# Retention in a hybrid decoder layer: q times the carried state as one f32 matmul, the mean of squares on ScalarE, and a third raw weight buffer filled half a pair ahead

## The chip, the cores and the metric

The kernel runs on one core of one Trainium2 chip. The metric is the device time of one execution in microseconds (us), as the median of the runs of a kernel. The engines are named as in the profile: PE is TensorE, PEld its weight load, DVE is VectorE, ACT is ScalarE, POOL is GpSimd, SP is SyncE, which issues DMAs; each engine works through its own instructions in the order in which they stand.

## What is computed

The reference is one inference step of a layer with a windowed attention, a retention branch, a gated merge and a convolutional FFN, on a prompt of 1024 tokens and a group of 8 sequences with 4 new tokens each. The change lies in the retention branch and in the product with `w_in` that feeds it. Per head (4 of them, keys of 128, values of 256) and per block of 128 tokens:

```python
h = xn @ w_in                      # q, k, v, gates of all branches: the columns are split after
scores = einsum('bihd,bjhd->bhij', q, k) * dmask
inner  = einsum('bhij,bjhe->bihe', scores, v)
cross  = einsum('bihd,bhde->bihe', q, s0) * q_decay      # q times the carried state
s_new  = exp(log_g * L) * s0 + einsum('bjhd,bjhe->bhde', k * k_decay, v)
o      = inner + cross;  o = o * rsqrt(mean(o * o) + EPS)
```

The new tokens of the 8 sequences go through the same formula with a state of their own that comes from memory (`state_ret`) and goes back to it (`ret_sample`).

## The kernel before

All data are float32. Nearly every product is made from two-part operands of the type f32r: `split(hi, lo, src)` (L227) writes `hi`, a cast on ACT (L228), and `lo = src - hi` (L223 where DVE does it, L225 where POOL does), and `mm3` (L254 to 257) issues three matmuls, hi by hi, hi by lo, lo by hi. A few small products are f32 matmuls without a split; the trace shows each of those as two records.

Nothing in the change touches the first 290 us (norm, attention) or what follows about 700 us (merge, `w_o`, FFN). In between two streams of work run through each other:

- **The stream** (`stream`, L874). It makes 16 column pairs of `w_in` one after the other, by a Strassen-Winograd scheme: 7 products of 12 matmuls for each half `j` of the tokens, 14 a pair. A pair's raw weights are two loads of 512 KB, in `pair_weights` (L335; the DMAs are L340), the first holding a11 and a12, the second a21 and a22. `in_split` (L857) forms the sums (`s1` and `a21`, on DVE in L223) and splits all seven operands (`w_split`, L323: cast on ACT in L329, rest on DVE). The raw buffers come from the pool `wraw` with two buffers. `in_split` of the next pair is started, that is its loads are issued, at A22 of a pair's first half, and its operands are asked for one by one during the second half. Products leave PSUM by ACT (L898) and by two adds on DVE (L921, L923, tile `pair`).
- **The retention of the samples** (`sample`, L991), four heads, about 300 to 440 us. Per head it handles 8 states in 4 blocks of two: `load_s0` (L984; DMA L989) fetches a block, `split` makes `s0s`, four matmuls use it, `kb` (L1033) and L1035 make the update, L1036 adds it on DVE in place, and POOL issues the store (L1038). `load_s0` is called two blocks ahead of use, with four buffers.
- **The retention of the prompt**, 32 blocks `g` (4 heads of 8 blocks), about 440 to 700 us. `front` (L1108) makes k by q and turned k in `ps_a` (L1113, L1114), masks and splits the scores (`sT`), scales k (`kt`), splits `v` (`vt`) and, in all blocks but a head's first, splits q (`qs`, cast on ACT, rest on POOL). `middle` (L1130) adds scores by v and q by state in `ps_b` and makes k by v in `ps_a`; L1144 makes the new state on DVE, and the state is split (`sts`, ACT and DVE) for the next block. `finish` (L970) squares the output with a sum (L971, ACT), takes mean and eps on DVE (`ms`, L280), the power -1/2 on POOL (`rs`, L282), and scales on ACT (L973). `tail` (L1155) turns it by two matmuls (L979) and multiplies the gate in (L1163, DVE).

The code says in which order these are written (`adv(n)` takes n steps of the stream between two pieces of retention); the final order of each engine's instructions is set by a scheduler at build, which places them by its own estimates of durations. The loads of `w_raw`, of the states and of q and k stand in one queue, SP's, in a fixed order: a load that waits for its buffer holds all loads behind it.

Of the kernel before, what the change touches and what calls it, by code (L numbers as in the profile page):

```python
# [9 lines left out]
F32 = mybir.dt.float32  # L10
F32R = mybir.dt.float32r
U32 = mybir.dt.uint32
AF = mybir.ActivationFunctionType
# [5 lines left out]
P = 128  # L19
# [101 lines left out]
def trunk(ctx, tc, I, O):  # L121
# [645 lines left out]
    pb = ppool("pb", 2, ps_stack)  # L767
    wx["sum"], wx["raw"] = pool("wsum", 1, stack=sm_stack), wraw
    p2 = pool("p2", 1, stack=ph_stack)
# [38 lines left out]
    def ST(name, shape, dt=F32, **kw):  # L808
        return rp.tile(list(shape), dt, name=name, **kw)
# [64 lines left out]
    def stream():  # L874
# [3 lines left out]
        next(ws)  # L878
        ops = {p: next(ws) for p in early}
        last, nh = None, 0  # L880
        for i, n in enumerate(ORDER):
            for j in range(2):
# [17 lines left out]
                for p in (A11, S1, A22, S2, A12, S4, S3):  # L900
                    if p == A22:
                        if last is not None:
                            product(A22, *last)
                        if j == 0:
                            ops[A22] = next(ws)
                            if i + 1 < len(ORDER):
                                ws = in_split(ORDER[i + 1])
                                next(ws)
                        if last is not None:
                            yield  # L910
                        continue
# [14 lines left out]
                    if j and i + 1 < len(ORDER):  # L926
                        nxt[p] = next(ws)
                    yield
                last = bk[1], ops[A22], j, dst
# [37 lines left out]
    def finish(po, n, s, h, bufs=2):  # L967

        ssq = sml.tile([P, 1], F32, name="ss")[:n]
        o = ST("o", (P, 256), bufs=bufs)[:n]  # L970
        S.activation(o, po[:n, :256], AF.Square, accum_out=ssq)  # L971
        r = rsqrt_mean(ssq, 256, n, 1, oeps[:n, s, h:h + 1])
        S.mul(o, po[:n, :256], r)  # L973
        return o
# [9 lines left out]
    def load_s0(n):  # L984
        if n >= 2 * DB:
            return
        h, bb = n // 4, 2 * (n % 4)
        s0s_[n] = ST("s0", (P, 2, 256), bufs=4)
        ld.dma_start(out=s0s_[n], in_=I["state_ret"][0, bb:bb + 2, h].rearrange("b k e -> k b e"))  # L989

    def sample(h):  # L991
        gS = float(GAMMA[h] ** 4)
        dm = ST("dm", (P, P), bufs=2)
        ld.dma_start(out=dm, in_=I["dmask"][:, h, 1])
# [5 lines left out]
        for i in range(2):  # L1000
            S.copy(out=r8[:, i, :].rearrange("p (o t) -> p o t", o=4), in_=rep(qk8[:, i]))
        v8 = ST("v8", (P, 256), F32R, bufs=2)
        S.copy(out=v8[0:32], in_=vs)
# [17 lines left out]
        for bb in range(0, DB, 2):  # L1021
            s0 = s0s_[(h * DB + bb) // 2]
            load_s0((h * DB + bb) // 2 + 2)
            s0s = ST("s0s", (P, 2, 2, 256), F32R)
# [19 lines left out]

    for n in range(2):
        load_s0(n)
    adv(18)
# [60 lines left out]
    def front(g, dm):  # L1108
# [14 lines left out]
        split(vt[:, 0], vt[:, 1], f32(vt[:, 1]))  # L1123
        qs = None
        if tt:
            qs = ST("qs", (P, 2, P), F32R, bufs=2)
            split(qs[:, 0], qs[:, 1], q, G)
        return ps, sT, kt, vt, qs

    def middle(g, ps, sT, kt, vt, qs):  # L1130
        h, tt = divmod(g, NB)
# [5 lines left out]
        if tt:  # L1137
            sts = state["sts"]
            mm3(po, qs[:, 0], qs[:, 1], sts[:, 0], sts[:, 1], False, True)
        pk = ps[:, 256:]  # L1140
# [580 lines left out]
```

## Time and profile before

| what | value |
|---|---|
| median of 3 runs | 1690.79 us (1689.51 to 1692.35) |
| the profiled execution | 1689.79 us, its span 1688.0 us |
| mean granted clock of TensorE | 0.992 |
| busy over the span: PE, DVE, ACT, POOL | 97%, 75%, 52%, 30% |
| PE instructions | 12643 |

The span runs from the first to the last instruction; 1.79 us of the profiled execution lie outside it. Granted clock is what the throttle gave TensorE as a share of full speed. In the rows of the profile, `x28` is a count, three durations are minimum, median and maximum in ns, and `[1.66 <-DVE pair L921]` says that the engine stood idle for 1.66 us until that instruction of another engine had ended.

### The profile page before, as it was taken

To read this page: it belongs to the slowest core of one execution; us is meant where nothing else is said; L and a number is where in the kernel's file an instruction comes from. 1 tells how busy PE (TensorE), PEld (TensorE's weight loads), DVE (VectorE), ACT (ScalarE), POOL (GpSimd) and SP (SyncE) were. 2 spreads that over 40 slices of the span, in tenths; PEclk is the share of its full clock that TensorE was granted. 3 is DMA by queue.
4 is the path that set the end of the run, shared out by engine and by line. 5 is a ranking of instruction groups with operands and counts; after the bars stand their busy time and mean duration, and the time that the engine had idled before them with its cause. 6 is when DMAs were issued, how large, how long until landed. Compare 5 with 4: busy or idle time off the path is not lost.

```text
span 1688.0 us, 32984 instructions
## 1 busy us (share of the span) xinstructions
PE 1633.9 (97%) x12643; PEld 1591.9 (94%) x12643; DVE 1273.3 (75%) x2227; ACT 870.0 (52%) x1942; POOL 499.1 (30%) x714
## 2 busy tenths in 40 slices
PE   8999999888989999999899999999999999999997
PEld 7999989888989989999778999999999999999997
DVE  7887737799677777658857888888888888445476
ACT  6566534444656665564433555555555556444343
POOL 4232420356344443341312122212313323111101
PEclk9999999999999999999999999999999999999999
DMA  7212222435777677596721244454444447866655
GB/s 198 66 45 73 82 63 103 147 124 168 225 230 230 202 246 222 194 296 205 229 94 68 64 141 159 150 161 148 152 146 146 146 146 254 256 184 201 196 175 157
DMA packets 273295, 273.92 MB, mean 162 GB/s; under 512 B 23040, under 2 KB 234272, under 8 KB 273121
## 3 DMA queue, kind: packets, MB, share of 16 engines
q1 hardware_dynamic: 239377, 155.25, 31.7%
q0 software_dynamic: 33760, 116.57, 19.9%
q8 instruction: 99, 1.62, 0.4%
q14 instruction: 59, 0.48, 0.1%
HBM read 184.24 MB, written 87.49 MB: 161 GB/s over the span
## 4 chain that ended last, share of the span: by engine, by line
PE 74%; DVE 9%; DMA 8%; issue 3%; ACT 3%; POOL 1%; SPq 0%; DVEq 0%; ACTq 0%; POOLq 0%
PE ps_m L256 9%; PE ps_m L257 9%; PE ps_m L255 9%; PE ps_t L256 7%; PE ps_t L255 7%; PE ps_t L257 7%; PE ps_q L255 3%; PE ps_q L257 3%; PE ps_q L256 3%; PE ps_mm L255 3%; PE ps_mm L256 3%; PE ps_mm L257 3%; DMA w_raw<-in_w_in 2%; DVE w L223 1%; DMA w_raw<-in_w_r_proj 1%
## 5 line engine op out<-in xcount | busy, mean ns | idle before, releaser
L255 PE MATMUL ps_q<-xh,w 128*128 128x264 f32 x512 | 150.6, 294 | 10.0 <-DVE pair L921 6.4
L223 DVE SCALAR_TENSOR_TENSOR w_lo<-w_raw,w_hi 128x1024 fp32r<-128x1024 f32 x83 | 104.8, 1268 | 65.8 <-ACT w_hi L228 61.3
L255 PE MATMUL ps_t<-xh,w_hi 128*128 128x264 f32 (+2 forms) x524 | 148.9, 284 | 0.0
L256 PE MATMUL ps_t<-xl,w_hi 128*128 128x264 f32 (+2 forms) x524 | 148.7, 284 | 0.0
L257 PE MATMUL ps_t<-xh,w_lo 128*128 128x264 f32 (+2 forms) x524 | 148.0, 283 | 0.0
L256 PE MATMUL ps_q<-xl,w 128*128 128x264 f32 x512 | 147.0, 287 | 0.0
L257 PE MATMUL ps_m<-xh,w_lo 128*128 128x264 f32 x512 | 145.5, 284 | 1.5 <-DVE w_lo L223 1.5
L257 PE MATMUL ps_q<-xh,w 128*128 128x264 f32 x512 | 146.3, 287 | 0.0
L255 PE MATMUL ps_m<-xh,w_hi 128*128 128x264 f32 x512 | 145.9, 285 | 0.0
L256 PE MATMUL ps_m<-xl,w_hi 128*128 128x264 f32 x512 | 145.5, 284 | 0.0
L223 DVE SCALAR_TENSOR_TENSOR w<-w_raw,w 128x512 fp32r<-128x512 f32 x152 | 110.3, 730 | 26.4 <-ACT w L329 25.3
L1471 DVE SCALAR_TENSOR_TENSOR c_out<-u_ext,fconst,c_out 128x1024 f32<-128x1024 f32 x96 | 122.0, 1281 | 2.6 <-ACT c_out L1467 0.5
L228 ACT CAST w_hi<-w_raw 128x1024 fp32r<-128x1024 f32 x62 | 65.2, 1051 | 107.0 <-PE ps_t L256 74.5
L255 PEld LDWEIGHTS ps_q<-xh,w 128*128 128x128 f32 x512 | 97.8, 191 | 12.9 <-DVE pair L921 8.4
L329 ACT CAST w<-w_raw 128x512 fp32r<-128x512 f32 x152 | 94.1, 621 | 27.0 <-DVE w_raw L223 15.1
L257 PEld LDWEIGHTS ps_t<-xh,w_lo 128*128 128x128 f32 x524 | 98.8, 188 | 0.0
L256 PEld LDWEIGHTS ps_t<-xl,w_hi 128*128 128x128 f32 x524 | 98.6, 188 | 0.0
L255 PEld LDWEIGHTS ps_t<-xh,w_hi 128*128 128x128 f32 x524 | 98.6, 188 | 0.0
L257 PEld LDWEIGHTS ps_m<-xh,w_lo 128*128 128x128 f32 x512 | 96.3, 188 | 1.9 <-DVE w_lo L223 1.9
L256 PEld LDWEIGHTS ps_q<-xl,w 128*128 128x128 f32 x512 | 97.9, 191 | 0.0
L257 PEld LDWEIGHTS ps_q<-xh,w 128*128 128x128 f32 x512 | 97.6, 191 | 0.0
L223 DVE SCALAR_TENSOR_TENSOR xl<-t,xh 128x1056 fp32r<-128x1056 f32 (+1 forms) x53 | 67.7, 1280 | 39.0 <-ACT xh L228 38.9
(468 smaller groups left out, 6233.2 us busy)
## 6 DMA issues: line engine op xcount, KB each, us to landing
w_raw<-in_w_up SPq DMA_DIRECT2D x48, 512.0 KB, 4.1
w_raw<-in_w_in SPq DMA_DIRECT2D x42, 512.0 KB, 4.6
w_raw<-s_d SPq DMA_DIRECT2D x60, 256.0 KB, 3.7
t_d<-t POOLq DMA_DIRECT2D x24, 528.0 KB, 4.1
t<-t_d POOLq DMA_DIRECT2D x24, 528.0 KB, 5.0
t<-in_w_down SPq DMA_DIRECT2D x40, 256.0 KB, 4.6
s_d<-t POOLq DMA_DIRECT2D x20, 512.0 KB, 3.7
w_raw<-in_w_down SPq DMA_DIRECT2D x36, 256.0 KB, 4.9
```

The costliest lines, as they stand in the source:

```text
L223: pinned(V.scalar_tensor_tensor(out=out, in0=in0, scalar=1.0, in1=in1, op0=mult, op1=op))
L228: pinned(S.copy(out=hi, in_=src))
L255: TE.matmul(ps, wh, xh, start=start, stop=False, **kw)
L256: TE.matmul(ps, wh, xl, start=False, stop=False, **kw)
L257: TE.matmul(ps, wl, xh, start=False, stop=stop, **kw)
L329: S.copy(out=t[:, 0:4], in_=src)
L1471: V.scalar_tensor_tensor(out=c[:, NS:], in0=u[:, g, NU + t:NU + t + SEQ], scalar=sc[t], in1=c[:, NS:], op0=mult, op1=add)
```

## The change

- The product of q and the carried state is one f32 matmul on the tiles `q` and `state` themselves; `qs`, `sts` and their splits are gone. That takes 84 f32r matmuls, 56 casts on ACT, 28 subtractions on DVE and 28 on POOL out, and puts 28 f32 matmuls in.
- In `finish` the squares are taken of a sixteenth of the values, so the sum is a mean over 256 already; eps is added by an ACT instruction in place of the one on DVE (36 of each). The power on POOL stays.
- Every third load of a `w_in` pair now lands in a buffer of the pool `wsum`, so there are three raw buffers. `in_split` is started for the pair after the next one, at S4 of a pair's second half, and once more before the loop.
- In `sample`, `s0` has three buffers instead of four and is fetched one block ahead instead of two; `dm` and `v8` have one buffer instead of two.

```diff
-    wx["sum"], wx["raw"] = pool("wsum", 1, stack=sm_stack), wraw
+    wx["sum"] = wx["raw"] = pool("wsum", 1, stack=sm_stack)
...
+        coming = in_split(ORDER[1])
+        next(coming)
...
                         if j == 0:
                             ops[A22] = next(ws)
-                            if i + 1 < len(ORDER):
-                                ws = in_split(ORDER[i + 1])
-                                next(ws)
+                            ws = coming
...
                     if j and i + 1 < len(ORDER):
                         nxt[p] = next(ws)
+                        if p == S4 and i + 2 < len(ORDER):
+                            coming = in_split(ORDER[i + 2])
+                            next(coming)
...
-        S.activation(o, po[:n, :256], AF.Square, accum_out=ssq)
-        r = rsqrt_mean(ssq, 256, n, 1, oeps[:n, s, h:h + 1])
+        S.activation(o, po[:n, :256], AF.Square, scale=1 / 16, accum_out=ssq)
+        ms = sml.tile([P, 16], F32, name="ms")[:n, :1]
+        S.activation(ms, ssq, AF.Identity, bias=oeps[:n, s, h:h + 1])
+        r = sml.tile([P, 16], F32, name="rs")[:n, :1]
+        G.tensor_tensor(out=r, in0=ms, in1=mhalf[:n, :1], op=ALU.pow)
...
-        s0s_[n] = ST("s0", (P, 2, 256), bufs=4)
+        s0s_[n] = ST("s0", (P, 2, 256), bufs=3)
...
-        dm = ST("dm", (P, P), bufs=2)
+        dm = ST("dm", (P, P))
...
-        v8 = ST("v8", (P, 256), F32R, bufs=2)
+        v8 = ST("v8", (P, 256), F32R)
...
-            load_s0((h * DB + bb) // 2 + 2)
+            load_s0((h * DB + bb) // 2 + 1)
...
-    for n in range(2):
-        load_s0(n)
+    load_s0(0)
...
-        qs = None
-        if tt:
-            qs = ST("qs", (P, 2, P), F32R, bufs=2)
-            split(qs[:, 0], qs[:, 1], q, G)
-        return ps, sT, kt, vt, qs
+        return ps, sT, kt, vt, q
...
-            sts = state["sts"]
-            mm3(po, qs[:, 0], qs[:, 1], sts[:, 0], sts[:, 1], False, True)
+            TE.matmul(po, q, state["s"], start=False, stop=True)
...
-        if tt < NB - 1:
-            sts = state["sts"] = ST("sts", (P, 2, 256), F32R)
-            split(sts[:, 0], sts[:, 1], ns_)
-        else:
+        if tt == NB - 1:
```

The scheduler's order differs from about 290 to 700 us on every engine, and nowhere else. Three places follow, each before and then after.

SP's queue where the stream begins: `w_raw` are the raw weights of the first pairs, `rcos` and `rsin` the tables of the rotation, `s_` the first sample states. Before:

```order
L340 DMA w_raw<-in_w_in 128x8x128
L956 DMA oeps<-in_oeps 128x8
L956 DMA kdec<-in_kdec 128x8
L340 DMA w_raw<-in_w_in 128x8x128 x3
L949 DMA rcos<-in_rcos 128x1056
L950 DMA rsin<-in_rsin 128x1056
L956 DMA bm<-in_bm 128x8
L989 DMA s_3562<-in_state_ret 128x2x256
L989 DMA s_3564<-in_state_ret 128x2x256
```

After:

```order
L340 DMA w_raw<-in_w_in 128x8x128
L959 DMA oeps<-in_oeps 128x8
L959 DMA kdec<-in_kdec 128x8
L340 DMA w_raw<-in_w_in 128x8x128 x4
L952 DMA rcos<-in_rcos 128x1056
L953 DMA rsin<-in_rsin 128x1056
L959 DMA bm<-in_bm 128x8
L995 DMA s_3562<-in_state_ret 128x2x256
L1000 DMA dm<-in_dmask 128x128
```

Five weight loads instead of four stand ahead of the tables, and one state load instead of two behind them.

DVE at the same place: `w_` are split operands, `s_3699` (after: `s_3697`) is the second pair's `s1`, `pair` the adds of the products (L921, L923). Before:

```order
L223 SCALAR_TENSOR_TENSOR w_3586<-w_raw,w_3586 128x512
L923 TENSOR_TENSOR pair<-ps_q_3596,pair 128x264
L223 SCALAR_TENSOR_TENSOR w_3700<-w_raw,w_3700 128x512
L921 TENSOR_TENSOR pair<-ps_q_3595,pair 128x264
L223 SCALAR_TENSOR_TENSOR s_3699<-w_raw 128x512
L822 STREAM_SHUFFLE sh<-pair 128x528
L223 SCALAR_TENSOR_TENSOR w_raw<-w_raw 128x512
```

After:

```order
L223 SCALAR_TENSOR_TENSOR w_3584<-w_raw,w_3584 128x512
L223 SCALAR_TENSOR_TENSOR s_3697<-w_raw 128x512
L923 TENSOR_TENSOR pair<-ps_q_3598,pair 128x264
L223 SCALAR_TENSOR_TENSOR w_raw<-w_raw 128x512
L223 SCALAR_TENSOR_TENSOR w_3698<-w_raw,w_3698 128x512
L921 TENSOR_TENSOR pair<-ps_q_3597,pair 128x264
L822 STREAM_SHUFFLE sh<-pair 128x528
```

The sums over the second pair's raw weights moved ahead of both adds on the first pair's products.

PE at the prompt's sixth block, with `ps_b<-vt,sT` scores by v, `ps_a<-vt,kt` k by v, `ps_a<-qk` k by q, `ps_q` the stream's products and L979 the turning of an output. Before, from the product of the fifth state on:

```order
L255 MATMUL ps_b<-vt,sT 128x256
L256 MATMUL ps_b<-vt,sT 128x256
L257 MATMUL ps_b<-vt,sT 128x256
L255 MATMUL ps_b<-sts,qs 128x256
L256 MATMUL ps_b<-sts,qs 128x256
L257 MATMUL ps_b<-sts,qs 128x256
L256 MATMUL ps_q_5959<-xl,w_5894 128x264
L257 MATMUL ps_q_5959<-xh,w_5894 128x264
L979 MATMUL ps_b<-ident,o 128x128 x2
L1113 MATMUL ps_a<-qk 128x128
L1114 MATMUL ps_a<-ident,qk 128x128
L255 MATMUL ps_a<-vt,kt 128x256
```

After:

```order
L255 MATMUL ps_b<-vt,sT 128x256
L256 MATMUL ps_b<-vt,sT 128x256
L257 MATMUL ps_b<-vt,sT 128x256
L1139 MATMUL ps_b<-state,qk 128x256
L255 MATMUL ps_a<-vt,kt 128x256
L256 MATMUL ps_a<-vt,kt 128x256
L257 MATMUL ps_a<-vt,kt 128x256
L255 MATMUL ps_b<-vt,sT 128x256
L256 MATMUL ps_b<-vt,sT 128x256
L257 MATMUL ps_b<-vt,sT 128x256
L1139 MATMUL ps_b<-state,qk 128x256
L255 MATMUL ps_a<-vt,kt 128x256
```

The three matmuls on `sts` and `qs` became the one of L1139. Two blocks now follow each other with no matmul of the stream between them, while before the stream's matmuls stood between one block and the next.

More of the change, by code (lines that the diff above doesn't have):

```diff
@@ L1123, in front, with middle @@
         split(vt[:, 0], vt[:, 1], f32(vt[:, 1]))
-        qs = None
-        if tt:
-            qs = ST("qs", (P, 2, P), F32R, bufs=2)
-            split(qs[:, 0], qs[:, 1], q, G)
-        return ps, sT, kt, vt, qs
-    def middle(g, ps, sT, kt, vt, qs):
+        return ps, sT, kt, vt, q
+    def middle(g, ps, sT, kt, vt, q):
         h, tt = divmod(g, NB)
```

## The prediction

> **What bounds the kernel now.** I read the page first, then busy times by stage, then what PE waits for in the stretch that the change reorders, then the places behind the largest of those waits.
>
> ```profile
> PE 1633.9 (97%) x12643; PEld 1591.9 (94%) x12643; DVE 1273.3 (75%) x2227; ACT 870.0 (52%) x1942; POOL 499.1 (30%) x714
> ```
>
> PE is busy for 97% of the span, so what can be won is the rest and the matmuls themselves. The stages, with the columns from, to, length, busy PE, PEld, DVE, ACT, POOL (instructions), granted clock, DMA share, GB/s:
>
> ```profile
> 290.00:420.00 130.00, 115.78 (x874) 110.91 (x873) 112.91 (x187) 52.93 (x129) 66.46 (x56) 0.97 0.44 144
> 420.00:700.00 280.00, 267.89 (x2155) 262.78 (x2154) 203.92 (x519) 166.55 (x457) 117.06 (x188) 0.99 0.70 221
> 320.00:360.00 40.00, 36.82 (x277) 36.05 (x277) 37.90 (x67) 16.22 (x44) 20.89 (x17) 0.93 0.42 136
> 360.00:400.00 40.00, 36.38 (x279) 33.94 (x278) 39.64 (x66) 17.58 (x47) 26.29 (x23) 1.00 0.43 138
> 480.00:520.00 40.00, 36.88 (x282) 35.95 (x282) 30.16 (x79) 23.54 (x67) 20.44 (x35) 0.91 0.71 223
> ```
>
> The affected 410 us hold two regimes. From 320 to 400 us, with the samples, DVE is full (37.90 and 39.64 of 40 us) and PE waits for it. From 420 on, DVE has slack on average (203.92 of 280) and PE waits now and then. Beside that, the granted clock costs 7% of 40 us (2.8 us) and 9% of 40 us (3.6 us) in two slices. PE's waits between 290 and 700 us (total, times, longest):
>
> ```profile
> PE ps_q L255 <- DVE pair L921: 6.4, 8, 1.7
> PE ps_a L1035 <- DVE kb L1033: 4.5, 5, 1.6
> PE ps_a L1113 <- DVE state L1144: 4.0, 3, 2.1
> PE ps_q L255 <- ACT pair L898: 3.7, 4, 1.3
> PE ps_b L979 <- ACT o L973: 2.7, 4, 0.9
> PE ps_q L255 <- DVE pair L923: 2.6, 2, 1.9
> ```
>
> These six sum to 23.9 us. That is the ceiling for everything the change does to waits; the halved clock could add some 6 us. Four of the six end on DVE, so the reader should ask what holds DVE there. One such place, DVE and then PE:
>
> ```profile
> 525.84 0.21 DVE L280 TENSOR_SCALAR ms<-ss,oeps 128x1 f32<-128x1 f32 x1
> 528.31 0.69 DVE L223 SCALAR_TENSOR_TENSOR s<-w_raw 128x512 f32<-128x512 f32 x1 [2.27 <-DMA w_raw<-in_w_in]
> 528.92 0.42 DVE L223 SCALAR_TENSOR_TENSOR sts<-state,sts 128x256 fp32r<-128x256 f32 x1
> 529.26 0.69 DVE L223 SCALAR_TENSOR_TENSOR w_raw<-w_raw 128x512 f32<-128x512 f32 x1
> 529.86 0.43 DVE L921 TENSOR_TENSOR pair<-ps_q,pair 128x264 f32<-128x264 f32 x1
> 530.34 0.39 PE L255 MATMUL ps_q<-xh,w 128*128 128x264 f32 x1 [1.66 <-DVE pair L921]
> ```
>
> PE's row names L921, but L921 was only queued: ahead of it DVE stood 2.27 us for a raw weight load, then did three other operations. The chain of waits has that load as its piece:
>
> ```profile
> 523.31 4.98 DMA w_raw<-in_w_in
> ```
>
> **Part 1: one f32 matmul for q times state.** The operations that go, by tile, and the durations that I use for the matmul:
>
> ```profile
> L228 ACT CAST sts<-state x28: 402/406/418, 462.8 to 691.6; 128x256 fp32r<-128x256 f32 x28
> L223 DVE SCALAR_TENSOR_TENSOR sts<-state,sts x28: 409/420/736, 463.7 to 692.0; 128x256 fp32r<-128x256 f32 x28
> L228 ACT CAST qs<-qk x28: 284/296/322, 454.3 to 684.2; 128x128 fp32r<-128x128 f32 x28
> L225 POOL TENSOR_TENSOR qs<-qk,qs x28: 447/475/1354, 454.7 to 684.6; 128x128 fp32r<-128x128 f32 x28
> 488.24 0.38 PE L1113 MATMUL ps_a<-qk 128*128 128x128 f32 x2
> 488.46 0.27 PE L1114 MATMUL ps_a<-ident,qk 128*128 128x128 f32 x1
> 488.70 0.28 PE L255 MATMUL ps_a<-vt,kt 128*128 128x256 f32 x1
> 488.81 0.28 PE L256 MATMUL ps_a<-vt,kt 128*128 128x256 f32 x1
> 488.93 0.28 PE L257 MATMUL ps_a<-vt,kt 128*128 128x256 f32 x1
> ```
>
> On PE, f32r matmuls of 256 columns start 0.115 to 0.12 us apart, so three cost 0.35. The f32 matmul of 128 columns is a pair of records: 0.38 for both against 0.27 for one, so they start 0.11 apart, and the next instruction starts 0.22 after the first. Twice the columns, twice that: 0.44. The product becomes dearer by 0.09 us, 28 x 0.09 = **+2.5 us**, all of it on the busiest engine. Bounds: if each of the two passes ran at the f32r pace, 2 x 0.118 = 0.24, -3.1 us; if each took its whole recorded 0.28, 0.56, +5.9 us. I take 0.44 since the row is the same kind of matmul.
>
> The Trainium skill, "FP8 and Floating Point Precision", section TensorE Precision Notes, counts a true FP32 product as four passes where the rounded form reads once, which speaks against replacing three matmuls by one: by it 4 x 0.118 = 0.47, and this term would be +3.4 us (an estimate). No row here has 256 columns in f32; the pair of L1113 is near the rule, for its two records are 0.11 apart at half the columns.
>
> On the others: DVE loses 28 x 0.420 = 11.8 us, ACT 28 x (0.406 + 0.296) = 19.7 us, POOL 28 x 0.475 = 13.3 us. None of these bounds, so the removal counts only through waits (part 2).
>
> **Part 2: the mean of squares on ACT.** What goes from DVE, and who waits in that chain:
>
> ```profile
> L280 DVE TENSOR_SCALAR ms<-ss,oeps x36: 195/208/217, 360.6 to 699.0; 128x1 f32<-128x1 f32 x32, 32x1 f32<-32x1 f32 x4
> ACT o L973 <- POOL rs L282: 10.2, 12, 2.3
> ```
>
> DVE loses 36 x 0.208 = 7.5 us. ACT gains 36 small instructions; I take the same 0.21 us, so 7.6 us (bounds from half of it to the cast's 0.406, 4 to 15 us), less than the 19.7 that part 1 took from it. The sum no longer stands behind DVE's queue on its way to POOL.
>
> Together DVE has 19.3 us less of 203.9, mostly in 420 to 700 us. The waits that this can shorten are those on the state (4.0) and on the scaled output (2.7). Both are chains of several engines, and only the queueing in them shrinks; I take a bit under half, **-3 us**, bounds 0 and -6.7. It could turn into a loss where blocks now follow each other on PE without cover (the sixth and seventh): 14 matmuls of the stream stood between them, 14 x 0.12 = 1.7 us, and without them PE waits for state and output once more, 2 to 3 us with the update (0.42) and the steps of `finish`. Before, this neighbourhood already cost a wait of that size and the slow clock of 480 to 520, so I set it off against those.
>
> **Part 3: third raw buffer, loads half a pair ahead.** The loads take 4.6 us to land in the median, and DVE waits for them:
>
> ```profile
> w_raw<-in_w_in SPq DMA_DIRECT2D x42, 512.0 KB, 4.6
> DVE s L223 <- DMA w_raw<-in_w_in: 15.0, 9, 3.0
> ```
>
> Nine waits, 15.0 us of DVE. A load that is issued half a pair (14 products x 12 matmuls x 0.12 / 2 = 10 us) earlier is there in time by more than its 4.6 us. What DVE's wait is worth on PE is read at 528: 2.27 became 1.66. Not every one lands on PE; the rows to which it can belong are those on L921 and L923, 6.4 + 2.6 = 9.0 us, the bound. I take a bit under half, **-4 us**, bounds 0 and -9. What is late next is L898 on ACT (3.7 us), which the change leaves.
>
> At the start of the stream the sums over the second pair now stand ahead of both adds:
>
> ```profile
> 301.66 0.43 DVE L923 TENSOR_TENSOR pair<-ps_q,pair 128x264 f32<-128x264 f32 x1 [1.32 <-PE ps_q L257]
> 307.77 0.69 DVE L223 SCALAR_TENSOR_TENSOR s<-w_raw 128x512 f32<-128x512 f32 x1 [3.04 <-DMA w_raw<-in_w_in]
> ```
>
> The 3.04 us of idle DVE come right before the stretch where DVE is full, so less of it moves all that follows forward; against that, L923, and with it the product that needs its bank, is now queued behind a load. SP's five loads instead of four delay the tables little, for the added buffer is free and its load has no wait. **-1 us**, bounds -3 and +1.5.
>
> **Part 4: what pays for the buffer.** A state block is fetched one block ahead with three buffers. The load for block m+1 now needs the store of block m-2 where it needed that of m-3. The third head's updates, and SP's waits for such stores:
>
> ```profile
> 409.06 0.68 DVE L1036 SCALAR_TENSOR_TENSOR s<-s,ps_a 128x512 f32<-128x512 f32 x1
> 413.05 0.67 DVE L1036 SCALAR_TENSOR_TENSOR s<-s,ps_a 128x512 f32<-128x512 f32 x1
> 417.06 0.68 DVE L1036 SCALAR_TENSOR_TENSOR s<-s,ps_a 128x512 f32<-128x512 f32 x1
> SPq L989 <- DMA out_ret_sample<-s: 40.4, 10, 9.8
> out_ret_sample<-s POOLq DMA_DIRECT2D x12, 256.0 KB, 3.1
> s<-in_state_ret SPq DMA_DIRECT2D x16, 256.0 KB, 2.7
> ```
>
> Update 0.7, store 3.1, load 2.7 and, as an estimate, 1.2 us for what waits in POOL's and SP's queues make 7.7 us from an update to the next load in its buffer. Two blocks are 8.0 us apart here: it just fits, with nothing to spare where there were 4 us. I take **+1 us**, bounds -3 (other order, same work) and +6 (rival 2).
>
> **Part 5: the clock.** The 2.8 and 3.6 us of lost clock come with the gaps; if gaps go, some of it goes. **-1.5 us**, bounds 0 and -6.4.
>
> Sum: +2.5 - 3 - 4 - 1 + 1 - 1.5 = **-6.0 us** on the profiled 1689.8 (span 1688.0 and 1.8 outside it). That execution lies 1.0 below the median of the runs, so I put it on the median: 1690.8 - 6.0 = **1684.8 us**. The forecast's own range is -10 to -3.
>
> **The rivals.** A measurement here can tell about 0.2%, 3.4 us, from no change.
>
> 1. *The gain stays in the queues.* SP's loads stand in one queue, and a load of q and k whose buffer is taken holds `w_raw` behind it, however many buffers there are:
>
> ```profile
> SPq L1084 <- PE ps_a L1114: 67.0, 22, 7.9
> ```
>
> Then part 3 gives -1, not -5, the freed DVE time stays idle time (-1, not -3), and parts 1, 4 and 5 (+2.5 + 1 - 1) make about 0: 1691 us. For it: 22 such waits. Against: the order puts the weight loads earlier in that queue.
>
> 2. *Slower: the states come late.* If store and load take 10 instead of 7.7 us (SP's longest wait was 9.8), each block waits 2 us from a spacing of 8.0 for two blocks on; DVE, which PE waits for there, loses about 1 us a block, 8 us over the last two heads, and the weight loads behind SP's wait are late as well, so part 3 gives -3. With +2.5 from part 1 and -2 from part 2, 1690.8 + 5.5 = about 1696 us. It decides from the point where the turn of a buffer takes more than two blocks' spacing. Against it: in the first two heads the spacing is wider, since DVE is full.
>
> 3. *More is won.* If all waits on L921 and L923 go (-9), those on state and output go (-6.7) and the clock comes back by half (-3), with +2.5 and +1: -15, 1676 us. For it speaks that delays on in-order queues add up. The Trainium skill, "SBUF — State Buffer", section Who interferes with whom, says that a DVE instruction with two SBUF inputs contends with a GpSimd instruction that reads SBUF; by it each of POOL's 28 removed subtractions could also have held DVE for up to its 0.475 us, 13 us of DVE. The trace agrees in one row: 736 ns at most for an `sts` subtraction whose median is 420.
>
> **How the numbers follow.** Forecast 0.48, rival 1 0.22, rival 2 0.18, rival 3 0.12. Of the forecast about 0.05 falls inside 3.4 us. So faster 0.43 + 0.12 = 0.55, same 0.22 + 0.05 = 0.27, slower 0.18. The range leaves out rival 3's far half and rival 2's far half, 0.15, and reaches from 1675 to 1696 us.
>
> **What would show it.** In the profile after: L1139's records 0.2 to 0.23 us apart (part 1 right); DVE's wait for `w_raw` down from 15.0 to under 5 us and PE's on L921 and L923 from 9.0 to about 5 (part 3); PE's waits on state and output below 6.7 together (part 2). ACT or DVE waiting for `in_state_ret` over 3 us would mean rival 2; SP still letting `w_raw` go late, rival 1. The forecast is wrong if 440 to 700 us takes as long as before.

## The result and the profile after

The changed kernel is slower: 1702.43 us (median of 8 runs, 1697.56 to 1709.54) against 1689.74 (8 runs, 1686.78 to 1692.35), a ratio of 1.0077 with a 95% interval of 1.0058 to 1.0095, some 13 us. The time lies above the predicted range. The profiled execution of the changed kernel took 1698.26 us; it is the second fastest of the eight and shows only 8.2 us of span more than before (1696.2 against 1688.0), so the size of the whole loss is taken from the timed runs, and the places from the profile.

```profile
PE 1633.4 (96%) x12615; PEld 1591.4 (94%) x12615; DVE 1255.0 (74%) x2163; ACT 867.6 (51%) x1922; POOL 487.1 (29%) x686
```

DVE lost 18.3 us of work, as the prediction worked out (19.3), POOL 12.0, and PE's busy time is the same. The work went as planned; the span did not follow. Where the time went is seen from when each thing happens. k turned (the transpose in `front`, 32 blocks) and the last of the stream's products, in the kernel before and then after ("456.3 to 686.8" are the first and the last start in us):

```profile
L1114 PE MATMUL ps_a<-ident,qk x32: 271/273/421, 456.3 to 686.8; 128*128 128x128 f32 x32
L257 PE MATMUL ps_q<-ex,w x256: 278/284/392, 291.7 to 726.0; 128*128 128x264 f32 x128
```

```profile
L1119 PE MATMUL ps_a<-ident,qk x32: 272/272/421, 463.5 to 693.5; 128*128 128x128 f32 x32
L257 PE MATMUL ps_q<-ex,w x256: 278/285/473, 291.8 to 732.9; 128*128 128x264 f32 x128
```

Both start the stream together, the prompt's first block comes 7.2 us later, and both streams of work end 6.7 to 6.9 us later. So most of the 8.2 us arise between 290 and 730 us, and they show first at the first head. PE there, three slices of 40 us (their columns as in the prediction), before and then after:

```profile
440.00:480.00 40.00, 38.22 (x311) 37.36 (x311) 27.74 (x70) 25.48 (x70) 15.59 (x26) 1.00 0.72 227
480.00:520.00 40.00, 36.88 (x282) 35.95 (x282) 30.16 (x79) 23.54 (x67) 20.44 (x35) 0.91 0.71 223
520.00:560.00 40.00, 37.32 (x305) 36.55 (x303) 29.47 (x77) 22.38 (x63) 17.61 (x28) 1.00 0.83 263
```

```profile
440.00:480.00 40.00, 37.52 (x296) 37.06 (x295) 22.63 (x52) 24.23 (x61) 11.62 (x19) 0.96 0.59 190
480.00:520.00 40.00, 32.08 (x240) 30.70 (x239) 26.44 (x69) 21.58 (x62) 17.55 (x28) 0.96 0.75 228
520.00:560.00 40.00, 39.52 (x322) 39.10 (x321) 28.42 (x69) 24.15 (x64) 13.86 (x22) 1.00 0.80 253
```

In the slice from 480 PE is busy for 32.08 us where it was 36.88: nearly 5 us are lost in the first head's later blocks, and some 2 of them come back in the slice from 520. PE's waits after, between 290 and 720 us:

```profile
PE ps_a L1118 <- DMA qk<-qk_d: 8.4, 3, 5.3
PE ps_q L255 <- DVE pair L921: 4.9, 4, 1.8
PE ps_a L255 <- DVE kt L1126: 2.6, 2, 1.4
PE ps_a L1118 <- DVE state L1144: 2.4, 3, 1.3
PE ps_q L255 <- DVE pair L923: 2.1, 2, 1.9
PE ps_b L985 <- ACT o L979: 1.3, 1, 1.3
```

The waits the change was to shorten did shrink: on state and scaled output together 3.7 us after 6.7, on L921 and L923 7.0 after 9.0. A wait that the profile of before did not show at all, on the loads of q and k, is larger than all of that.

The first of these three waits goes back to SP's queue, before and then after:

```profile
435.22 2.86 SPq L1084 DMA_DIRECT2D qk<-qk_d  x3
452.30 0.37 SPq L340 DMA_DIRECT2D w_raw<-in_w_in  x1
```

```profile
453.57 0.37 SPq L340 DMA_DIRECT2D w_raw<-in_w_in  x1
454.04 3.60 SPq L1089 DMA_DIRECT2D qk<-qk_d  x3
```

A weight load that must wait for its buffer until 453.57 now stands ahead of the first three q/k loads, which are issued 19 us later than before. PE pays 2.48 us at once, and 5.29 in a later block:

```profile
462.94 0.77 PE L1118 MATMUL ps_a<-qk 128*128 128x128 f32 x2 [2.48 <-DMA qk<-qk_d]
496.68 0.77 PE L1118 MATMUL ps_a<-qk 128*128 128x128 f32 x2 [5.29 <-DMA qk<-qk_d]
```

That second load stands in SP's queue behind the loads of the table `w_down`, which wait for a buffer, and DVE stands for the same table:

```profile
489.24 1.37 SPq L292 DMA_DIRECT2D zt<-in_w_down  x2
490.66 1.21 SPq L1089 DMA_DIRECT2D qk<-qk_d  x2
```

```profile
496.10 1.35 DVE L223 SCALAR_TENSOR_TENSOR zt<-zt 128x256 f32<-128x256 f32 x3 [5.66 <-DMA zt<-in_w_down]
```

```profile
DVE s L223 <- DMA w_raw<-in_w_in: 29.1, 12, 5.5
```

The last line, of DVE's waits from 290 to 720 us, bears on part 3 of the prediction: DVE's wait for raw weights nearly doubled, from 15.0 to 29.1 us, with three buffers and earlier loads.

### The profile page after: what moved, and what is told of

Same layout as the page of the kernel before. It is cut to its first block, busy times and chain, and to the rows that moved or that the text cites. A ratio compares the mean times of both kernels' runs of the same rounds, so it can differ in the third digit from the quotient of the medians.

```text
span 1696.2 us, 32758 instructions
## 1 busy us (share of the span) xinstructions
PE 1633.4 (96%) x12615; PEld 1591.4 (94%) x12615; DVE 1255.0 (74%) x2163; ACT 867.6 (51%) x1922; POOL 487.1 (29%) x686
## 4 chain that ended last, share of the span: by engine, by line
PE 56%; DMA 9%; DVE 5%; issue 4%; ACT 2%; POOL 1%; SPq 0%; DVEq 0%; POOLq 0%; ACTq 0%
PE ps_m L256 8%; PE ps_m L257 8%; PE ps_m L255 8%; PE ps_t L256 7%; PE ps_t L255 7%; PE ps_t L257 7%; PE ps_q L257 2%; PE ps_q L255 2%; PE ps_q L256 2%; DMA qk<-qk_d 1%; DMA vt<-v_d 1%; DMA t<-z_d 1%; DMA g_in<-gm_d 1%; DMA zt<-in_w_r_proj 1%; DVE w L223 1%
## 5 line engine op out<-in xcount | busy, mean ns | idle before, releaser
L255 PE MATMUL ps_q<-xh,w 128*128 128x264 f32 x512 | 149.3, 292 | 7.5 <-DVE pair L921 4.9
L255 PE MATMUL ps_t<-xh,w_hi 128*128 128x264 f32 (+2 forms) x524 | 149.0, 284 | 0.0
L256 PE MATMUL ps_t<-xl,w_hi 128*128 128x264 f32 (+2 forms) x524 | 148.7, 284 | 0.0
L256 PE MATMUL ps_q<-xl,w 128*128 128x264 f32 x512 | 147.0, 287 | 0.0
L255 PE MATMUL ps_m<-xh,w_hi 128*128 128x264 f32 x512 | 145.9, 285 | 1.1 <-ACT w_hi L228 1.1
L256 PE MATMUL ps_m<-xl,w_hi 128*128 128x264 f32 x512 | 145.4, 284 | 0.0
L223 DVE SCALAR_TENSOR_TENSOR w<-w_raw,w 128x512 fp32r<-128x512 f32 x152 | 106.8, 707 | 32.3 <-ACT w L329 29.8
L255 PEld LDWEIGHTS ps_q<-xh,w 128*128 128x128 f32 x512 | 97.2, 190 | 9.5 <-DVE pair L921 5.8
L256 PEld LDWEIGHTS ps_t<-xl,w_hi 128*128 128x128 f32 x524 | 98.6, 188 | 0.0
L255 PEld LDWEIGHTS ps_t<-xh,w_hi 128*128 128x128 f32 x524 | 98.6, 188 | 0.0
L256 PEld LDWEIGHTS ps_q<-xl,w 128*128 128x128 f32 x512 | 97.5, 191 | 0.1
```

Source lines behind the costliest of these rows:

```text
L223: pinned(V.scalar_tensor_tensor(out=out, in0=in0, scalar=1.0, in1=in1, op0=mult, op1=op))
L255: TE.matmul(ps, wh, xh, start=start, stop=False, **kw)
L256: TE.matmul(ps, wh, xl, start=False, stop=False, **kw)
```

## The experiments

Each was timed in five rounds against the kernel before on the same chip. Times are given as ratio to it with the 95% interval; 0.1% is 1.7 us. Three theories stood at the start. The **queue theory**: the loss is PE's wait for q/k loads that stand behind other loads in SP's queue. Its rivals: the **lifetime theory** (the f32 product reads q itself, so q/k buffers are held longer) and the **price theory** (the f32 matmul).

**1 to 4: which part brings it.** Experiment 1 has only the first item of the change, 2 only the second:

```diff
-            mm3(po, qs[:, 0], qs[:, 1], sts[:, 0], sts[:, 1], False, True)
+            TE.matmul(po, q, state["s"], start=False, stop=True)
```

```diff
-        r = rsqrt_mean(ssq, 256, n, 1, oeps[:n, s, h:h + 1])
+        S.activation(ms, ssq, AF.Identity, bias=oeps[:n, s, h:h + 1])
```

Experiment 3 has both, and 4 is the changed kernel with the loads issued where they were before (third buffer kept).

> Only the f32 product of q and state; the rest as before. Queue theory (the loss is PE waiting for q/k loads that stand behind weight and table loads in SP's queue): the first three q/k loads keep their place ahead of the weight load, so no wait at the first block; -3 to +4 us against the kernel before, with PE's waits for qk_d under 2 us. Lifetime theory (the product reads q itself, so a q/k buffer is held until the product and the next q/k load is late): +5 us or more, PE waits for qk_d over 4 us, and SP's waits for a q/k buffer name the product. Price theory (the f32 matmul itself): +2.3 us, evenly spread over 28 places of 0.08.

Measured: 1.0017 (1.0007 to 1.0027), +2.9 us. One wait for q/k of 2.1 us.

> Only the mean of squares on ACT; the rest as before. Queue theory: the order that this edit alone brings has a weight load ahead of the first three q/k loads, so PE waits 2 to 3 us at the first block; +2 to +6 us. Lifetime and price theories: no f32 product, so nothing lost; -3 to 0 us.

Measured: 1.0032 (1.0018 to 1.0045), +5.4 us; the q/k loads are late as expected. The profiled execution is the fastest of the twelve (1689.71, no slower than the kernel before), so the late loads alone need not cost time.

> The f32 product and the mean of squares on ACT, without the third raw buffer, the early loads and the smaller sample buffers. Queue theory: the same order of q/k and weight loads at the first block as in the changed kernel, so most of the loss is here, +5 to +13 us. A theory that lays the loss on the third buffer and what pays for it: within 3 us of the kernel before.

Measured: 1.0079 (1.0064 to 1.0094), +13.3 us: as slow as the whole change, with two raw buffers and the old sample buffers. The two items together cost more than their sum (8.3).

> The changed kernel with weights loaded at the old place, the third buffer kept. Queue theory: the order on SP's queue is nearly that of the changed kernel, so the time is too, +8 to +15 us against the kernel before. A theory that lays the loss on the early loads: back to the kernel before within 3 us.

Measured: 1.0045 (1.0029 to 1.0061), +7.6 us, just below the expected band. DVE's wait for raw weights is nearly as long as in the changed kernel (25.2 against 29.1 us), though no load is issued earlier:

```profile
DVE s L223 <- DMA w_raw<-in_w_in: 25.2, 10, 4.2
```

So a loss of this size needs neither the third buffer nor the small sample buffers. The lifetime theory finds little in experiment 1, and the price theory cannot account for 13 us.

**5 to 7: are the two holds at the first head the cause?** On experiment 3, since it has the loss and free memory: a third buffer for `zt` (5), the first three q/k loads from POOL's queue (6), and both (7).

```diff
-        y = ST("zt", (P, T), bufs=2)
+        y = ST("zt", (P, T), bufs=3)
...
-        ld.dma_start(out=qks[g], in_=qk_d[h]
+        (st if g < 3 else ld).dma_start(out=qks[g], in_=qk_d[h]
```

> f32 product and mean of squares on ACT (as the third experiment, +13.3 us), with three buffers in place of two for the tile zt. Table theory (DVE's queue stands 7.3 us on the w_down tables, which wait for a zt buffer, and PE 4.7 us behind that): the wait at 487 to 495 us goes, 5 to 7 us of the loss with it, +6 to +8 us against the kernel before. Lifetime theory (q/k buffers held by the f32 product): no change, +12 to +14 us.

Measured: 1.0062 (1.0042 to 1.0083), +10.5 us. DVE's wait for `w_down` fell from 9.9 to 1.9 us, but one for `gm_d` of 4.9 took its place, with PE 5.1 us behind it.

> The third experiment with the first three q/k loads issued by POOL, so that they no longer stand in SP's queue behind a weight load that waits 15.6 us for its buffer. Queue theory: the first head starts at 456 us as before in place of 461, PE's wait of 2.2 us for q/k goes, and 4 to 7 us of the loss with it: +6 to +9 us. Lifetime theory: no change, +12 to +14 us.

Measured: 1.0062 (1.0046 to 1.0078), +10.5 us. PE's wait for q/k is gone (4.1 us in experiment 3); its waits on L921 from 440 us on are 5.2 in place of 3.4 us. The edit did less than it was meant to: POOL issues the three loads at 450.6 to 453.7 us, where SP issues them from 451.4 us in experiment 3 and from 435.2 us in the kernel before, and the first block still comes late, at 460.8 us (456.3 before):

```profile
L1117 PE MATMUL ps_a<-ident,qk x32: 272/273/421, 460.8 to 693.3; 128*128 128x128 f32 x32
```

> Both of these edits on the third experiment. Queue and table theory together: what is left is the price of the f32 product, 0 to +3 us against the kernel before. If the two holds are only where the same time shows up, and the loss is in the order of PE itself: +8 us or more.

Measured: 1.0065 (1.0043 to 1.0088), +11 us. Each hold shrank in its own run and another took its place, and here PE even waits 4.0 us for q/k loads: the two holds are not the whole loss. None of 5, 6 and 7 differs from experiment 3 by more than the intervals. That the loads are late at all was not tested by 6 and 7, since POOL issues them no earlier (from 452.7 us in 7); experiment 17 comes back to it. The expectation then lays the loss on the order of PE.

**8: the mean of squares back on DVE, all else changed.**

> The changed kernel with the mean of squares back on DVE; f32 product, third buffer, early loads and small sample buffers stay. If the move to ACT is what brings the late first head: within 3 us of the kernel before. If any denser order of the first head does it: +7 to +13 us, with DVE standing over 4 us on the w_down tables.

Measured: 1.0102 (1.0082 to 1.0122), +17 us, the slowest of all. So it is not the move to ACT alone.

What these kernels have in common was found in the order of their instructions. In the code, 48 matmuls of the stream belong to each block. Counted in each kernel's order on PE, the stream's matmuls that stand before the end of k by v of block 0, and then between one block's and the next one's:

```
kernel               block 0, then 1 to 10                              ratio
before               1073  8 37 28 36 38   6  72  48  48  48            1
1  f32 product       1073  8 34 10 40 37  24  36  84  48  48            1.0017
2  mean on ACT       1100 14 52 22 35  3   0  72  48  48  48            1.0032
5  3 with zt x3      1100 14 35 11 41 14  11   0 120  48  48            1.0062
after                1102  9 37 12 42 14  10   0 120  48  48            1.0077
3  both              1100 14 35 11 41 10  15   0   0 168  48            1.0079
4  after, old place  1102  9 37 12 42 14  10   0 120  48  48            1.0045
7  3, zt x3, POOL    1115 12 32 20 25 22   0   0 120  48  48            1.0065
6  3, q/k by POOL    1115 12 32 20 25 22   0   0   0   0 216            1.0062
8  after, DVE mean   1130 11 43 17 25  0   0   0   0   0 216            1.0102
9  after, 9 ahead    1125 17 42 30 48 48  48  48  48  48  48            1.0015
10 before, 9 ahead   1092 26 48 24 72 48  48  48  48  48  24            0.9961
```

Wherever the first block starts late against the stream (1100 to 1130 in place of 1073; in 9 and 10 the code itself moves the stream ahead), the order catches up by a **string**: two or more blocks with nothing between them. In the changed kernel these are blocks 6 and 7. The string is no full measure of the time: 6 has a string of five blocks and loses no more than the changed kernel with its two; and 4 has the same string as the changed kernel, and their intervals only touch (to 1.0061, from 1.0058), so the early loads may cost something of their own. That gave a fourth theory, the **string theory**: in a string PE stands open to every hold on DVE, ACT or a load, since no matmul of the stream covers it.

**9 to 12: remove the string, and make one.** Nine stream steps more are called before the prompt's first block and nine fewer at the end (9, on the changed kernel; 10, on the kernel before). In 11 and 12, also on the kernel before, PE's matmuls of the first ten blocks are kept in the order of the code as well (the `held` line), 48 to a block; in 12 that order has a string (48, 48, 48, 24, 0, 0, 0, 24, 180).

```diff
+    adv(9)
     coming, behind = ahead(0), None
...
-    adv(len(ORDER) * 14 - 8 - 78 - 4 * NBLK - 1)
+    adv(len(ORDER) * 14 - 8 - 78 - 4 * NBLK - 1 - 9)
```

```diff
-        TE.matmul(ps, wh, xh, start=start, stop=False, **kw)
+        held(TE.matmul(ps, wh, xh, start=start, stop=False, **kw))
...
+        late = 4 <= g < 8
-        adv(2)
+        adv(0 if late else 2)
         m = middle(g, *f)
-        adv(1)
+        adv(0 if late else 1)
...
-        adv(1)
+        adv(17 if g == 8 else 0 if late else 1)
```

> The changed kernel with nine stream steps (9 products) moved ahead of the prompt's first block and taken from the end. The first three q/k loads still stand behind a weight load, but the scheduler no longer has blocks to catch up with: at least 17 stream matmuls stand between any two blocks, where the changed kernel has 10, 0 and then 120. String theory (the loss is PE waiting inside a string of blocks that stand without stream matmuls): the loss goes, -4 to +4 us against the kernel before. Queue theory: the late q/k loads stay and so does the loss, +8 us or more.

Measured: 1.0015 (1.0005 to 1.0025), +2.5 us: 10.5 us less than the changed kernel, and the late q/k loads are still there (PE waits 2.5 us for them).

> The kernel before with the same nine steps moved. It had one short string only (6 matmuls at one block). String theory: 0 to 5 us faster than the kernel before, since those 5.8 us of waits around 490 us go in part. If moving the nine steps is worth as much by itself as on the changed kernel (not by way of the string): 8 us or more faster.

Measured: 0.9961 (0.9948 to 0.9974), -6.6 us: between the two expectations. This is the control of experiment 9, and it takes most of that gain away from the string. The nine steps win 10.5 us on the changed kernel and 6.6 on the kernel before, whose order has no string, only places with little cover (8 and 6 matmuls). Only the difference of some 4 us can be laid on the changed kernel's string, and with these four intervals it is uncertain by as much.

> The kernel before with nine steps moved and PE's order of the first ten blocks held to the order of the code: 48 stream matmuls at each block. String theory: within 4 us of the kernel before. This is the partner of the next one.

Measured: 0.9987 (0.9975 to 1.0000), -2.2 us. It is 4.4 us slower than experiment 10, though neither has a string, so the order has other effects of this size.

> As the one before, with a string made on purpose: three blocks with no stream matmul between them, and 180 after. All work, tiles and splits are those of the kernel before. String theory: 8 to 13 us slower than its partner, 2 to 3 us a block, with PE's waits in those blocks on state, scaled output and kt. If the loss of the changed kernel comes from the f32 product or the buffers and not from the string: within 3 us of the partner.

Measured: 1.0039 (1.0025 to 1.0054), +6.6 us against the kernel before, and 0.52% or 8.8 us against its partner (9.7 between the medians, 1695.49 and 1685.80). So on the instructions of the kernel before, with no f32 product and no third buffer, a string of four blocks alone costs some 9 us. The same DVE wait in the partner (first) and with the string, and what PE made of it:

```profile
496.06 0.89 DVE L223 SCALAR_TENSOR_TENSOR zt<-zt 128x256 f32<-128x256 f32 x2 [4.82 <-DMA zt<-in_w_down]
480.00:520.00 40.00, 36.69 (x296) 35.61 (x295) 27.85 (x73) 24.90 (x68) 18.31 (x30) 1.00 0.73 228
```

```profile
496.85 0.88 DVE L223 SCALAR_TENSOR_TENSOR zt<-zt 128x256 f32<-128x256 f32 x2 [5.33 <-DMA zt<-in_w_down]
498.32 0.80 PE L1119 MATMUL ps_a<-qk 128*128 128x128 f32 x2 [5.85 <-DVE state L1150]
480.00:520.00 40.00, 31.35 (x200) 28.49 (x200) 26.47 (x78) 19.48 (x64) 21.19 (x35) 0.79 0.69 212
```

DVE stands for the table load some 5 us in both. In the partner PE has the stream's products to work on and its busy time stays at 36.69; in the string it waits 5.85 us for a state that is queued on DVE behind that load, and the granted clock in the slice is 0.79 where the partner has 1.00, at most 0.21 x 40 = 8.4 us. The two losses are not to be added, since the clock does not matter while PE stands idle: PE has 96 matmuls fewer in the slice, as an estimate 11.5 us at the 0.12 us that one takes, for wait and clock together. Over whole runs the clock is lower too: 0.989 in the mean of five runs, 0.994 in the partner's twelve.

**13 to 18: what is left without a string.** With nine steps ahead the changed kernel is still 0.54%, 9.1 us, behind the kernel before with nine steps ahead, and neither has a string. So most of the 13 us does not come from the string. None of the six kernels that follow has one either; the fewest matmuls of the stream between two of their blocks are 9, in 18. On that footing: the f32 product alone (13), the mean on ACT alone (14), both (15); 16 is experiment 9 with the table sums on POOL; 17 is 15 with the mean on ACT in the prompt and on DVE in the samples; 18 is 9 with the mean on DVE.

> Only the f32 product, on the kernel with nine steps ahead (no string in it: 26 or more stream matmuls between blocks). Price theory (28 x 0.08 us and nothing else once strings are gone): 2 to 3 us above the kernel before with nine steps ahead, so -4 to -2 us against the kernel before. Load theory (a freer DVE is made to stand before loads that have not landed, with the state behind them): 4 us or more above it, DVE's waits for loads well over the 33.7 us of that kernel.

Measured: 0.9965 (0.9950 to 0.9980), -5.9 us, level with the kernel before with nine steps ahead (0.9961).

> Only the mean of squares on ACT, nine steps ahead. Price theory: within 1.5 us of the kernel before with nine steps ahead, -7 to -4 us against the kernel before. Queue theory: the first q/k loads stand behind a weight load again, 2 to 4 us above it.

Measured: 1.0026 (1.0010 to 1.0043), +4.4 us, 11 us above it. More than either theory gave.

> f32 product and mean of squares on ACT, nine steps ahead, two raw buffers. Price theory: 2 to 3 us above the kernel before with nine steps ahead. If the third buffer and the sample buffers make most of the 7.6 us by which the changed kernel with nine steps stays behind: below -2 us against the kernel before; if they make nothing: +1 to +4 us.

Measured: 1.0001 (0.9989 to 1.0014), level with the kernel before, between the two expectations. Against 13 the move to ACT costs 6 us.

> The changed kernel with nine steps ahead, and the twelve sets of four table sums (w_r and w_down, tile zt) on POOL in place of DVE, so that DVE no longer stands before those loads (13.3 + 5.9 us of its waits). Load theory: PE's wait on the state falls from 11.8 us to about 5, 3 to 6 us gained against that kernel, -4 to 0 us against the kernel before. Price theory: no gain, +1 to +4 us, or a loss where POOL holds DVE.

Measured: 1.0030 (1.0018 to 1.0042), +5.1 us. In the profiled execution PE's wait on the state fell, from 10.6 to 6.5 us between 440 and 720 us. That execution is the fastest of the twelve (1689.03 against a median of 1693.13), and the twelve together are no faster than experiment 9. So no time was won by it; whether the sums cost on POOL what their waits had cost on DVE was not told apart.

> The f32 product and nine steps ahead, with the mean of squares on ACT in the prompt's 32 blocks and on DVE in the four sample heads. With that alone the first three q/k loads stand ahead of the weight load again. Queue theory (the late first q/k loads cost the move to ACT its 6 us): as the f32 product alone with nine steps, -8 to -4 us against the kernel before, the first head at 455 to 457 us in place of 462. If ACT's longer chain in the prompt costs it: 0 to +3 us, as with all 36 on ACT.

Measured: 0.9982 (0.9970 to 0.9994), -3.0 us, halfway between 13 and 15. The diff:

```diff
+        if s:
+            S.activation(o, po[:n, :256], AF.Square, accum_out=ssq)
+            r = rsqrt_mean(ssq, 256, n, 1, oeps[:n, s, h:h + 1])
```

> The f32 product, third buffer, early loads and small sample buffers, mean of squares on DVE, nine steps ahead. In SP's queue a weight load stands ahead of the first three q/k loads. Queue theory: the first head late at 462 us or later, 0 to +5 us against the kernel before, so the third buffer takes back what the f32 product and the nine steps won. If only the move to ACT costs: -8 to -4 us.

Measured: 1.0000 (0.9989 to 1.0012), so the third buffer with its early loads and small sample buffers costs 0.35%, 5.9 us, on top of 13.

SP's queue before the first head in 13, 15 and 17, and in 18:

```profile
428.79 4.01 SPq L340 DMA_DIRECT2D w_raw<-in_w_in  x2
432.85 10.60 SPq L1084 DMA_DIRECT2D qk<-qk_d  x3
```

```profile
430.24 21.92 SPq L340 DMA_DIRECT2D w_raw<-in_w_in  x3
452.21 4.60 SPq L1087 DMA_DIRECT2D qk<-qk_d  x3
```

```profile
431.29 4.04 SPq L340 DMA_DIRECT2D w_raw<-in_w_in  x2
435.38 10.60 SPq L1092 DMA_DIRECT2D qk<-qk_d  x3
```

```profile
452.93 0.37 SPq L340 DMA_DIRECT2D w_raw<-in_w_in  x1
454.02 5.66 SPq L1086 DMA_DIRECT2D qk<-qk_d  x3
```

In 13 and 17 two weight loads stand ahead of the first three q/k loads, in 15 and 18 three, and the last of them waits some 20 us for its buffer. The first block follows, in the same four kernels:

```profile
L1114 PE MATMUL ps_a<-ident,qk x32: 272/272/273, 455.3 to 691.6; 128*128 128x128 f32 x32
```

```profile
L1117 PE MATMUL ps_a<-ident,qk x32: 272/273/421, 462.2 to 699.7; 128*128 128x128 f32 x32
```

```profile
L1122 PE MATMUL ps_a<-ident,qk x32: 272/273/273, 457.8 to 696.5; 128*128 128x128 f32 x32
```

```profile
L1116 PE MATMUL ps_a<-ident,qk x32: 272/273/421, 467.9 to 702.0; 128*128 128x128 f32 x32
```

The late q/k loads thus go with about half of the price of the move to ACT (17 against 15: 3 us) and with the loss in 18. The other half, 3 us between 13 and 17, was not settled. Both halves are at the edge of what can be told, since the intervals of 13, 17 and 15 overlap in turn, and 17 also moves the samples' own means back to DVE; so that the late loads are the cause is argued and not shown. Nor was it tried whether the third buffer is worth anything with the q/k loads ahead of the weights and no string.

## Why the prediction was wrong

A gain of 6 us was forecast and a loss of 13 was measured. The experiments without strings give each term its size: the f32 product with its relief of the other engines about nothing (13 against 10), the move to ACT 6 us lost (15 against 13), the third buffer with what pays for it 6 us lost (18 against 13), all together 9 us lost (9 against 10). The change's string brings the rest, some 4 us and uncertain. One step failed in parts 2 and 3 alike: work taken from DVE's queue, and slack given to a load, were counted as shorter waits, with the rest of the order left as it was. The new order took more than the shorter waits gave. How it took it is known in part only.

**Part 1, right.** The f32 product is what the pair of L1113 said. Its records, and PE around one of them:

```profile
L1139 PE MATMUL ps_b<-state,qk x56: 377/378/382, 473.4 to 704.3; 128*128 128x256 f32 x56
```

```profile
537.32 0.59 PE L1139 MATMUL ps_b<-state,qk 128*128 128x256 f32 x2
537.56 0.47 PE L255 MATMUL ps_a<-vt,kt 128*128 128x256 f32 x1
537.87 0.28 PE L256 MATMUL ps_a<-vt,kt 128*128 128x256 f32 x1
```

Two records start 0.59 - 0.38 = 0.21 apart; from L1139 to L256 it is 0.55 us, and less the 0.12 of L255 the product takes 0.43, against 0.44 predicted. Term: 28 x 0.08 = 2.2 us. Both the row and the four passes that the Trainium skill counts ("FP8 and Floating Point Precision", section TensorE Precision Notes; 0.47 by that rule) were near. Without strings the item costs nothing in all (13 against 10: 0.04%, inside the intervals), so something pays for the 2.2 us; its relief of DVE and ACT is the likely one.

**Part 2, where it failed.** The term was -3 us, and the two waits that it names fell by just that, from 6.7 to 3.7. In spite of it the move to ACT costs 6 us on top of the f32 product (15 against 13) and 11 us alone (14 against 10), with no string in any of the four. About half of the 6 goes with the first q/k loads, which the move puts behind a weight load; what the other half is stays open. The prediction looked at the chain of the mean itself and did not follow what the new order does to SP's queue at the first head.

The second step that failed is the offset. The prediction named two blocks that follow each other on PE without cover, priced them at 2 to 3 us, and set that off against waits and a slow clock that stood near there before, so it counted nothing. A string of four blocks costs some 9 us (12 against 11), since PE stands bare to DVE's 5 us hold for a load and the clock is lower there. The neighbourhood before did cost something, as the offset assumed, for the nine steps win 6.6 us there; but they win 10.5 on the changed kernel, so the offset was short by some 4 us, uncertain by as much. The cover was counted short as well: the 14 matmuls stood between q by state of block 6 and scores by v of block 7, and 60 more stood inside block 7, which the new order took away with them.

The Trainium skill, "TensorE: Matmul & The Clock Gate", section "HAM oscillation — how this bites in real kernels", says that waits between bursts of matmuls let the clock gate go back to half rate; the 0.79 of experiment 12 against 1.00 in its partner fits that. The changed kernel's own profile does not show it in the slice from 480 to 520 us: 0.96, with a wait of 5.29 us, against 0.91 before.

The instruction on ACT was mis-sized by a little:

```profile
L976 ACT ACTIVATE ms<-ss,oeps x36: 283/295/322, 356.2 to 705.3; 128x1 f32<-128x1 f32 x32, 32x1 f32<-32x1 f32 x4
```

0.295 us where 0.21 was taken, 36 x 0.085 = 3.1 us of ACT, inside the bounds given.

**Part 3, wrong in sign.** -4 and -1 were predicted, with +1 in part 4 for what pays for the buffer; without strings the three together cost 5.9 us (18 against 13). The step that failed is that slack on the buffer becomes slack on DVE: DVE's wait for raw weights was to fall under 5 us, and it rose from 15.0 to 29.1. The order was read at one place only, the start of the stream, and there the forecast even came true:

```profile
302.89 0.69 DVE L223 SCALAR_TENSOR_TENSOR s<-w_raw 128x512 f32<-128x512 f32 x1 [2.45 <-DMA w_raw<-in_w_in]
303.61 0.43 DVE L923 TENSOR_TENSOR pair<-ps_q,pair 128x264 f32<-128x264 f32 x1
```

The sum starts at 302.89 in place of 307.77, yet DVE waits for it about as long (2.45 after 3.04), because the sum moved forward in DVE's queue with its load, and L923 is 2 us later for it. So at this place the load's consumer was brought forward as well. The earlier loads are not all of it: with the third buffer and the loads at their old place (4) DVE still waits 25.2 us. Why it waits so long with three buffers was not followed further; two kernels with two buffers, 6 and 7, also reach 27.3 and 24.2. Beside that the weight load stands ahead of the first q/k loads in SP's queue, 19 us of their time, at a place which the prediction's look at that queue did not reach. Either the third buffer with what goes with it (18, on top of the f32 product) or the move to ACT (2, 14) is enough to bring this order; the f32 product alone (1, 13) does not.

**Part 4 and rival 2.** No wait for `in_state_ret` appears among the waits of DVE or ACT from 290 to 440 us, and the stream is level with before at 440 us (890 of its matmuls in the profile from 290 us on, 891 before). The late states did not happen. The end was on the slower side, but by another mechanism than the rival's.

**Rival 1** had the queue right and the sign wrong: it feared q/k loads that hold back weights; a weight load held back q/k.

**Part 5, wrong in sign.** -1.5 us was predicted. The mean granted clock was 0.994 in the profiled execution after and 0.992 before, but over the eight runs after it was 0.990 to 0.994, with a mean of 0.992, where the kernel before has means of 0.993 to 0.994 in the rounds of the experiments. So no clock was won, and as an estimate from these means some 3 or 4 of the 13 us are clock that was lost.

## What to carry to other kernels

Where two streams of work are laced into each other, one covers the other's waits. After any edit, count in the new order how much of the one stands between the steps of the other: a late start of one stream was caught up here in a string without cover, and a string of four blocks alone cost some 9 us (12 against 11), more than the edits were forecast to win. In an in-order queue, look at what stands behind every load that moved, not only at the load. And give a repair its control: the nine steps that won 10.5 us on the changed kernel won 6.6 on the kernel before, so most of what they won was not the repair of the change. The kernel before with nine stream steps moved ahead of the first block is faster than both kernels, at 0.9961 (0.9948 to 0.9974); with the f32 product as well it is level with that (0.9965).

## What the runs showed of the hardware

An f32 matmul of 256 columns takes 0.43 us on PE against 0.35 for three f32r ones of the same size. One ACT instruction on 128x1 took 0.295 us, DVE's on the same shape 0.208. Where PE waited 5.85 us at once and then went on in short pieces, the granted clock was 0.79 over 40 us (experiment 12), and 1.00 in the partner without the string; that is at most 8.4 us, of which the part that fell into the wait cost nothing.
